# Turning twelve head outputs by 32x32 blocks through DRAM instead of TensorE transposes, in an RWKV-7 / HGRN2 mixer layer

## The chip, the cores and the metric

The kernel runs on one core of a Trainium2 chip. The metric is the device time of one execution in microseconds (us). The kernel before takes 1044.72 us, the median of 3 runs (1044.42 to 1045.22).

## What is computed

One layer of a streaming encoder over 512 frames of 2048 channels. One input projection feeds two groups of heads, their gated outputs are concatenated, and one output projection, a residual and a layer norm follow:

```python
proj = einsum('btd,dc->btc', x, w_in)            # 512 x 2048 by 2048 x 8320
rw = token_shift(proj[..., :RWKV_COLS], shift_mu)
o_rwkv = rwkv7(rw)      # 16 heads of 64 = 8 pairs: r, k, v, z, decay, a
o_hgrn = hgrn2(proj[..., RWKV_COLS:])    # 8 heads of 128: q, f, i, g
y = einsum('btc,cd->btd', concat([o_rwkv, o_hgrn]), w_out)
out = layer_norm(ALPHA * x + y) * ln_w + ln_b
```

The ends of the two branches matter here. In RWKV the recurrence's output `o` is normalized over each head of 64, scaled and shifted by `gn_w` and `gn_b`, gets a bonus `bv` added, and is multiplied by `silu(z)`. In HGRN2 the output is divided by its root mean square over the head of 128 and multiplied by `g_norm_w` and `silu(g)`. Everything is float32.

## The kernel before, in words

**Products.** A float32 product is made of three passes in the fp32r format: each operand is split into a high part and a rest, and `three` (L485) issues high by high, high by rest and rest by high, each 128x128 by 128x512, into one PSUM tile. The weights arrive as 156 blocks `wr` of 512 KB from `w_all`, two buffers; ACT makes the high part `wh` (L361) and DVE the rest `wl` (L371), half a block at a time, three buffers each. These products are the main stream of TensorE (PE in the profile). First come the units of the input projection in the order of `_order()`, then the output projection.

**Side work.** The recurrences run beside the main stream: after each product `three` calls `plan.pump()`, which looks at queues of Python generators (preparation and turning of a pair, groups, scans, finishes, HGRN heads, stores). Each generator yields one instruction at a time. `Plan` keeps an estimated clock for each engine and issues an instruction when its estimated inputs are ready; `room(...)` waits for a free buffer, `landed(...)` for operands that a PE instruction needs and for a free PSUM bank `mix`. The order that results is fixed when the program is built, each engine then runs its own part of it in order, waiting on semaphores where an input is late. So the planner's estimates set the order, and the chip's times only decide who waits. Side work on PE comes in two sorts: plain fp32 with all 128 rows and columns ("whole"), and small tiles ("narrow"); PE leaves the main stream for such a group and goes back to it.

**The ends, before.** `rwkv_finish(S, p)` for pair p normalizes the output `o_all`, a tile `t` with 128 frames by 4 blocks of 128 channels. Gating needs channels on the partitions, so four PE transposes (`tr`, L352, against the identity in `cst`) write it to a PSUM tile `po`. One DVE instruction `stt` (L380) makes `g = po * gn_w/2 + bv`; a Tanh, and two more, apply the gate z. `hgrn_out` ends in the same way: the normalized output `o2` (a `t` tile too) goes through four transposes to `pn`, and one `stt` makes `g = pn * (g_norm_w/2) * gate`. `put_gated` hands g on: for pairs 0 to 5 and heads 0 to 5 it is stored in DRAM (`spill<-g`) and read again for the output projection; pairs 6, 7 and heads 6, 7 stay in SBUF.

**Turning through DRAM.** The kernel has a second way to transpose, `turned(dst, src, tmp, rows)`, which it uses for `bk` and `v` in `rwkv_turn` and, for heads 0 to 5, for the keys in `hgrn_out`: DVE transposes each 32x32 block within itself (`dtr`, L390) into `tmp`; one DMA writes `tmp` to a DRAM tile `far`; `rows` DMAs read `far` back so that the blocks change places, each to 32 partitions. All these DMAs are issued by SyncE (SP) through `send` (L327), in one order with the weight loads. Before each the generator waits until the planner's SP clock is no more than 0.2 us ahead, and it counts 4 us for the write and 4 us for the last read. The result stands in the order "p (a c j)": block row a, block column c, 32 elements j, and was so far put in plain order by an ACT copy.

Of the kernel before, what the change touches and what calls it, by code (L numbers as in the profile page):

```python
# [11 lines left out]
ALU = mybir.AluOpType  # L12
# [3 lines left out]
P = 128  # L16
# [241 lines left out]
def mixer_kernel(ctx, tc, head, x_r, w_all, par, up, ln_wb, consts, hmask, out):  # L258
# [11 lines left out]
    def nm(s):  # L270
        uid[0] += 1
        return f"{s}{uid[0]}"
# [8 lines left out]
    def st(tag, shape, dt=F32):  # L281
        return spool.tile(shape, dt, tag=tag, name=nm(tag), bufs=BUFS[tag])

    def take(tag, shape=(P, T), dt=F32):

        if not plan.free(tag):
            raise RuntimeError(f"no room: {tag}")
        slot = min(plan.slots[tag])
        plan.slots[tag].remove(slot)
        if tag in PBUFS:  # L290
            t = ppool.tile(list(shape), dt, tag=tag, name=nm(tag), bufs=PBUFS[tag])
            plan.banks.add(t.tensor.name)
        else:
            t = st(tag, list(shape), dt)
        name = t.tensor.name
        plan.busy[name] = (slot[1], None)
        tags[name] = tag
        return t

    def drop(*tiles):  # L300
        for t in tiles:
            name = t.tensor.name
            plan.slots[tags.pop(name)].append((plan.used.get(name, plan.count), plan.busy[name][0]))

    def room(**need):

        return lambda: all(plan.free(tag, n) for tag, n in need.items())

    def has(S, *names):
        return lambda: all(n in S for n in names)  # L310

    def landed(*tiles, n=0):

        names = [getattr(t, "tensor", t).name for t in tiles]

        def test():
            now = plan.clock["pe"] + plan.LEAD
            if not plan.free("mix") or min(plan.slots["mix"])[1] + 0.15 > now:
                return False
            return all(n in plan.ready and plan.seen(n, "pe") <= now for n in names)  # L320

        test.batch = n
        return test

    def send(o, i, cost=0.44):

        nc.sync.dma_start(o, i)  # L327
        plan.clock["sp"] = max(plan.clock["sp"], plan.clock["pe"]) + cost


    def size(ap):
        n = 1
        for s in ap.shape[1:]:
            n *= s
        return n
# [15 lines left out]
    def tr(o, i):  # L351
        return Op([("pe", 0.11, lambda: pe.transpose(o, i, ident))], [i], [o])  # L352
# [14 lines left out]
    def dve_op(reads, o, f, n=None, per=0.00104, base=0.07):  # L367
        return Op([("dve", base + (n or size(o)) * per, f)], reads, [o])
# [10 lines left out]
    def stt(o, a, s, b, f1, f2):  # L379
        return dve_op([a, b], o, lambda: dve.scalar_tensor_tensor(o, a, s, b, f1, f2), per=0.00113,  # L380
                      base=0.085 if o.shape[0] == P else 0.25 if size(o) == C else 0.165)

    def red(o, i):
        return dve_op([i], o, lambda: dve.tensor_reduce(o, i, AX.X, ALU.add), size(i))
# [4 lines left out]
    def dtr(o, i):  # L389
        return dve_op([i], o, lambda: dve.transpose(o, i), per=0.0019)  # L390
# [25 lines left out]
    def blocks(t, n):  # L416

        return t.rearrange("p (a c j) -> p a c j", a=4, c=n)

    def turned(dst, src, tmp, rows=4):  # L420

        far = dpool.tile([P, rows, size(tmp) // rows], F32, tag=nm("far"), name=nm("far"))
        yield dtr(tmp.rearrange("p b c j -> p c b j"), src)
        yield lambda: by_now(tmp)
        yield lambda: plan.clock["sp"] <= plan.clock["pe"] + 0.2
        send(far, tmp.rearrange("p b c j -> p b (c j)"))
        there = plan.busy[tmp.tensor.name] = (plan.clock["sp"] + 4.0, "dma")
        for b in range(rows):
            yield lambda: there[0] <= plan.clock["pe"] and plan.clock["sp"] <= plan.clock["pe"] + 0.2
            send(dst(b).rearrange("i a c j -> i a (c j)"), far[:, b].rearrange("(a i) x -> i a x", a=4))  # L430
        plan.ready[dst(0).tensor.name] = (plan.clock["sp"] + 4.0, "dma")
# [58 lines left out]
    def by_now(t):  # L490

        n = t.tensor.name
        return n in plan.ready and plan.seen(n, "pe") <= plan.clock["pe"] + plan.LEAD
# [79 lines left out]
    HW0, HA0, HKA, HRK, HGW, HGB, HHW, HOKA = range(8)  # L573

    def hcol(i, p):

        return half[:, i, p : p + 1]
# [362 lines left out]
    def rwkv_finish(S, p):  # L940

        o_all = S["o"]
        yield room(sm=1, ksq=1)
        og = o_all.rearrange("p j (h i) -> p (j h) i", i=64)
        sm = take("sm", [P, 3, 8])
        sq = take("ksq", [P, 8, 64])
        yield red(sm[:, 0], og)
        yield ts(sm[:, 0], sm[:, 0], 1.0 / 64, None, ALU.mult)
        yield tt(og, og, sm[:, 0, :, None].to_broadcast([P, 8, 64]), ALU.subtract)
        yield act(sq, og, AF.Square)  # L950
        yield red(sm[:, 1], sq)
        yield ts(sm[:, 1], sm[:, 1], 1.0 / 64, GN_EPS, ALU.mult, ALU.add)
        yield rsqrt(sm[:, 2], sm[:, 1])
        yield tt(og, og, sm[:, 2, :, None].to_broadcast([P, 8, 64]))
        drop(sm, sq)
        yield has(S, "z", "bv")
        yield room(g=1, ksq=1)
        g = take("g")
        sz = take("ksq")
        z = S["z"]  # L960
        yield landed(o_all)
        po = take("mix")
        for j in range(4):
            yield tr(po[:, j * P : j * P + P], o_all[:, j])
        yield act(sz, z, AF.Tanh, scale=0.5)
        yield stt(g, po, hcol(HGW, p), S["bv"], ALU.mult, ALU.add)
        drop(po)
        yield stt(z, sz, 1.0, z, ALU.add, ALU.mult)
        yield stt(g, g, hcol(HGB, p), z, ALU.add, ALU.mult)
        drop(z, S["bv"], S["ot"], sz)  # L970
        put_gated(p, g)
# [17 lines left out]
    def tiles(t):  # L989
        return t.rearrange("p (c t) -> p c t", t=P)  # L990
# [110 lines left out]
    def hgrn_out(S, h, q, k, dt_, dg, tot, tots):  # L1101

        yield room(g=1)
        g = take("g")
        kt = state = tiles(k)[:, 0:3]
        if h < 6:
            yield room(ksq=1)
            tmp = take("ksq")
            g4 = blocks(g[:, : 3 * P], 3)
            yield from turned(lambda b: g4[32 * b : 32 * b + 32], kt, blocks(tmp[:, : 3 * P], 3))  # L1110
            drop(tmp)
            yield act(kt.rearrange("p c (a j) -> p c a j", j=32), g4.rearrange("p a c j -> p c a j"), AF.Copy)
        else:
            yield landed(k)
            ps = take("mix")
            for t in range(3):
                yield tr(ps[:, t * P : t * P + P], k[:, t * P : t * P + P])
            yield copy(kt, tiles(ps)[:, 0:3])
            drop(ps)
        yield has(S, "i")  # L1120
        yield room(rs=1)
        i_all = S["i"]
        hs = slice(h % 4 * P, h % 4 * P + P)
        yield landed(i_all, k)
        ps = take("mix")
        for t in range(3):
            yield mm(ps[:, t * P : t * P + P], kt[:, t], i_all[:, t, hs])
        yield copy(state[:, 0], ps[:, :P])
        for t in (1, 2):
            yield stt(state[:, t], state[:, t - 1], tot[:, t : t + 1], ps[:, t * P : t * P + P], ALU.mult, ALU.add)  # L1130
        drop(ps, *tots)
        yield landed(dg, k, q)
        po = take("mix")
        for t in range(4):
            o = po[:, t * P : t * P + P]
            yield mm(o, dg[:, t], i_all[:, t, hs], stop=(t == 0))
            if t:
                yield mm(o, q[:, t * P : t * P + P], state[:, t - 1], start=False)
        o2 = q
        yield act(o2, po, AF.Square)  # L1140
        rs = take("rs", [P, 8])[:, :4]
        yield red(rs, tiles(o2))
        yield ts(rs, rs, 1.0 / P, 4.0 * RMS_EPS, ALU.mult, ALU.add)
        yield rsqrt(rs, rs)
        yield tt(tiles(o2), tiles(po), rs[:, :, None].to_broadcast([P, 4, P]))
        drop(po, k, dt_, rs)
        S["used"]()
        yield landed(o2)
        pn = take("mix")
        for j in range(4):  # L1150
            yield tr(pn[:, j * P : j * P + P], o2[:, j * P : j * P + P])
        yield has(S, "g")
        yield stt(g, pn, hcol(HHW, h), S["g"], ALU.mult, ALU.mult)
        drop(S["g"], pn, o2)
        put_gated(8 + h, g)

    def silu2(ps, put):
# [459 lines left out]
    for t in range(4):  # L1617
# [14 lines left out]
        for i in range(2):  # L1632
            c = slice(i * T // 2, i * T // 2 + T // 2)
# [85 lines left out]
```

## Time and profile before

| what | value |
|---|---|
| median of 3 runs | 1044.72 us |
| the profiled execution | 1044.08 us, span 1042.3 us |
| PE busy | 1033.4 us, 99% of the span |
| DVE busy | 760.9 us, 73% |
| ACT busy | 439.0 us, 42% |
| POOL busy | 42.4 us, 4% |
| granted PE clock | full in all 40 slices |
| DMA | 123.46 MB, 118 GB/s on average |

The span goes from the first to the last instruction; the execution's time is 1.8 us longer. In the rows of the profile a line such as `L485 PE MATMUL main<-xl,wh` names the source line, the engine, the operation and the tiles out<-in without their buffer numbers. PEld is the loading of the stationary operand, which overlaps PE. SPq is SyncE issuing DMAs. Matmuls are pipelined: one that is listed with 0.39 us is followed by the next after about 0.23 us, so the sum of their durations says less than the steps from start to start.

### The profile page before, as it was taken

How to read it: one execution, taken by the hardware profiler on the slowest of the kernel's cores; microseconds unless marked ns; L12 is line 12 of the kernel's file. 1: busy time of each engine (PE TensorE's matmuls, PEld its weight loads, DVE VectorE, ACT ScalarE, POOL GpSimd, SP SyncE). 2: the span in 40 equal slices, each digit the busy share in tenths (PEclk: the TensorE clock that was granted, in tenths of full speed). 3: DMA queues.
4: the chain of work that ended last, by engine and by line, in shares of the span. 5: the costliest groups of instructions: out<-in, count | busy, mean ns of one | idle time of the engine just before them, and what ended most of it. 6: DMA issues, size and time to landing. Idle time of an engine off the chain costs nothing.

```text
span 1042.3 us, 19372 instructions
## 1 busy us (share of the span) xinstructions
PE 1033.4 (99%) x7708; PEld 854.4 (82%) x7708; DVE 760.9 (73%) x1614; ACT 439.0 (42%) x816; POOL 42.4 (4%) x77
## 2 busy tenths in 40 slices
PE   9999999999999999999999999999999999999997
PEld 7888887888888888888888888888888888888885
DVE  7477987678679878678997656866997886525556
ACT  6445334545343355355243344534335444223321
POOL 0000001001000000100001000100001011000000
PEclk9999999999999999999999999999999999999999
DMA  9134432232434322234542323243532245445613
GB/s 334 52 94 133 148 116 84 77 112 71 137 107 147 122 63 88 76 106 141 151 130 82 91 71 110 92 121 113 152 101 69 77 161 185 143 129 161 207 58 131
DMA packets 48618, 123.46 MB, mean 118 GB/s; under 512 B 8720, under 2 KB 17424, under 8 KB 48400
## 3 DMA queue, kind: packets, MB, share of 16 engines
q1 hardware_dynamic: 48384, 122.03, 37.3%
q8 instruction: 60, 0.98, 0.4%
q14 instruction: 30, 0.25, 0.1%
q10 hardware_dynamic: 144, 0.20, 0.1%
HBM read 107.39 MB, written 14.81 MB: 117 GB/s over the span
## 4 chain that ended last, share of the span: by engine, by line
PE 94%; DVE 2%; ACT 1%; DMA 1%; issue 1%; SPq 0%; DVEq 0%; ACTq 0%
PE main L485 71%; PE mix L348 10%; PE mix L485 8%; PE main L1244 3%; PE main L348 1%; PE mix L352 1%; DVE wl L371 1%; DMA q<-head 0%; DMA q<-far 0%; DVE inv L380 0%; DVE inv L371 0%; DVE t L371 0%; ACT L362 0%; DVE big L390 0%; ACT t L362 0%
## 5 line engine op out<-in xcount | busy, mean ns | idle before, releaser
L485 PE MATMUL main<-xh,wl 128*128 128x512 f32 x864 | 340.9, 395 | 0.0
L485 PE MATMUL main<-xl,wh 128*128 128x512 f32 x864 | 339.8, 393 | 0.0
L485 PE MATMUL main<-xh,wh 128*128 128x512 f32 x864 | 339.8, 393 | 0.0
L361 ACT ACTIVATE wh<-wr 128x512 fp32r<-128x512 f32 x299 | 186.3, 626 | 228.6 <-PE main L485 159.3
L371 DVE TENSOR_TENSOR wl<-wr,wh 128x512 fp32r<-128x512 f32 x299 | 203.7, 683 | 75.9 <-ACT wh L361 74.1
L485 PEld LDWEIGHTS main<-xl,wh 128*128 128x128 f32 x864 | 162.3, 188 | 33.6
L485 PEld LDWEIGHTS main<-xh,wl 128*128 128x128 f32 x864 | 162.4, 188 | 33.0
L485 PEld LDWEIGHTS main<-xh,wh 128*128 128x128 f32 x864 | 162.4, 188 | 32.8
L485 PE MATMUL main<-wh,xh 128*128 128x512 f32 (+1 forms) x262 | 102.3, 390 | 0.2 <-ACT t L362 0.2
L485 PE MATMUL main<-wl,xh 128*128 128x512 f32 (+1 forms) x262 | 102.3, 391 | 0.0
L485 PE MATMUL main<-wh,xl 128*128 128x512 f32 (+1 forms) x262 | 102.1, 390 | 0.0
L485 PEld LDWEIGHTS main<-wh,xh 128*128 128x128 f32 x262 | 49.2, 188 | 10.7 <-ACT t L362 0.6
L485 PEld LDWEIGHTS main<-wl,xh 128*128 128x128 f32 x262 | 49.2, 188 | 10.1 <-DVE wl L371 0.3
L485 PEld LDWEIGHTS main<-wh,xl 128*128 128x128 f32 x262 | 49.2, 188 | 9.8
L362 ACT ACTIVATE t<-main,om 128x512 f32<-128x512 f32 x33 | 22.4, 685 | 56.8 <-PE main L485 46.5
L371 DVE TENSOR_TENSOR inv<-inv,inv 64x30 f32<-64x30 f32 (+14 forms) x120 | 38.5, 321 | 3.0
L371 DVE TENSOR_TENSOR inv<-inv 64x30 f32<-64x30 f32 (+14 forms) x120 | 38.4, 320 | 2.7
L361 ACT ACTIVATE t<-mix 64x128 f32<-64x128 f32 (+3 forms) x60 | 16.8, 280 | 53.7 <-DVE zz L371 25.6
L380 DVE SCALAR_TENSOR_TENSOR bd<-mix,pc,bd 64x64 f32<-64x64 f32 x112 | 31.7, 283 | 10.6 <-PE mix L348 8.5
L380 DVE SCALAR_TENSOR_TENSOR t<-main,pr,t 128x511 f32<-128x511 f32 x33 | 24.4, 745 | 20.4 <-ACT t L362 20.4
L371 DVE TENSOR_TENSOR t<-t,tot 128x256 f32<-128x256 f32 x96 | 37.2, 419 | 0.3
L362 ACT ACTIVATE t<-main 128x512 f32<-128x512 f32 x32 | 18.6, 595 | 36.9 <-PE main L485 36.8
(218 smaller groups left out, 1317.5 us busy)
## 6 DMA issues: line engine op xcount, KB each, us to landing
wr<-w_all SPq DMA_DIRECT2D x156, 512.0 KB, 3.6
q<-head SPq DMA_DIRECT2D x15, 448.0 KB, 5.9
far<-q SPq DMA_DIRECT2D x8, 512.0 KB, 5.1
q<-far SPq DMA_DIRECT2D x32, 128.0 KB, 3.6
g<-x_r SPq DMA_DIRECT2D x16, 256.0 KB, 4.0
spill<-g SPq DMA_DIRECT2D x12, 256.0 KB, 3.7
out<-q SPq DMA_DIRECT2D x12, 256.0 KB, 2.5
t<-spill SPq DMA_DIRECT2D x10, 256.0 KB, 4.1
```

What stands on the lines that cost most here:

```text
L348: return Op([("pe", cost, lambda: pe.matmul(o, l, r, start=start, stop=stop, **kw))], [l, r], [o], mode="narrow" if narrow else "main" if ...
L352: return Op([("pe", 0.11, lambda: pe.transpose(o, i, ident))], [i], [o])
L361: return "act", cost, lambda: sc_e.activation(o, i, f, scale=scale)
L362: return "act", cost, lambda: sc_e.activation(o, i, f, scale=scale, bias=bias)
L371: return dve_op([a, b], o, lambda: dve.tensor_tensor(o, a, b, f), base=0.16 if o.shape[0] < P and size(o) == C and o.tensor.name in tags e ...
L380: return dve_op([a, b], o, lambda: dve.scalar_tensor_tensor(o, a, s, b, f1, f2), per=0.00113, base=0.085 if o.shape[0] == P else 0.25 if s ...
L485: pe.matmul(ps, l, r, start=first and i == 0, stop=last and i == 2)
L1244: pe.matmul(pss[a], *ops, start=k == 0 and low == of == 0, stop=k == KT - 1 and low == 1)
```

## The change

For pairs 0 to 5 and heads 0 to 5 the four PE transposes are left out, and the PSUM tile with them. In their place `turned` moves the output through DRAM: one `dtr` of 128x512 on DVE into a buffer `ksq`, one DMA of 256 KB to `far`, four DMAs of 64 KB back, in pieces of 512 B, into the tile that held the output (`o_all` or `o2`). Gating reads the blocks where they lie: four `stt` of 128x128, one for each block row a, take the place of the one of 128x512, with a strided view of g and of the other operand. There is no ACT copy. Pairs 6, 7 and heads 6, 7 keep the old code.

```diff
@@ rwkv_finish
         drop(sm, sq)
+        far = p < 6
+        if far:
+            yield room(ksq=1)
+            tmp = take("ksq")
+            o4 = blocks(S["ot"], 4)
+            yield from turned(lambda b: o4[32 * b : 32 * b + 32], o_all, blocks(tmp, 4))
+            drop(tmp)
         yield has(S, "z", "bv")
         yield room(g=1, ksq=1)
         g = take("g")
         sz = take("ksq")
         z = S["z"]
-        yield landed(o_all)
-        po = take("mix")
-        for j in range(4):
-            yield tr(po[:, j * P : j * P + P], o_all[:, j])
+        if not far:
+            yield landed(o_all)
+            po = take("mix")
+            for j in range(4):
+                yield tr(po[:, j * P : j * P + P], o_all[:, j])
         yield act(sz, z, AF.Tanh, scale=0.5)
-        yield stt(g, po, hcol(HGW, p), S["bv"], ALU.mult, ALU.add)
-        drop(po)
+        if far:
+            c4, b4 = (t.rearrange("p (c a j) -> p c a j", a=4, j=32) for t in (g, S["bv"]))
+            for a in range(4):
+                yield stt(c4[:, :, a], o4[:, a], hcol(HGW, p), b4[:, :, a], ALU.mult, ALU.add)
+        else:
+            yield stt(g, po, hcol(HGW, p), S["bv"], ALU.mult, ALU.add)
+            drop(po)
@@ hgrn_out
-        yield landed(o2)
-        pn = take("mix")
-        for j in range(4):
-            yield tr(pn[:, j * P : j * P + P], o2[:, j * P : j * P + P])
-        yield has(S, "g")
-        yield stt(g, pn, hcol(HHW, h), S["g"], ALU.mult, ALU.mult)
-        drop(S["g"], pn, o2)
+        if h < 6:
+            yield room(ksq=1)
+            tmp = take("ksq")
+            o4 = blocks(o2, 4)
+            yield from turned(lambda b: o4[32 * b : 32 * b + 32], tiles(o2), blocks(tmp, 4))
+            drop(tmp)
+            yield has(S, "g")
+            c4, s4 = (t.rearrange("p (c a j) -> p c a j", a=4, j=32) for t in (g, S["g"]))
+            for a in range(4):
+                yield stt(c4[:, :, a], o4[:, a], hcol(HHW, h), s4[:, :, a], ALU.mult, ALU.mult)
+            drop(S["g"], o2)
+        else:
+...
```

The planner then makes another order. The rows below are those of the built programs, engine by engine; the number behind a tile's name is its buffer. At the first of the twelve places, about 216 us into the profiled execution, PE's order before is this (`t_961` is the normalized output of an HGRN head):

```order
L485 MATMUL main_2178<-xh_81,wl_2229 128x512
L485 MATMUL main_2178<-xh_82,wh_2228 128x512
L352 MATMUL mix_2300<-cst,t_961 128x128 x4
L485 MATMUL main_2178<-xl_98,wh_2228 128x512
L485 MATMUL main_2178<-xh_82,wl_2229 128x512
```

and with the change this:

```order
L485 MATMUL main_2178<-xh_81,wl_2229 128x512
L485 MATMUL main_2178<-xh_82,wh_2228 128x512
L485 MATMUL main_2178<-xl_98,wh_2228 128x512
L485 MATMUL main_2178<-xh_82,wl_2229 128x512
L485 MATMUL main_2178<-xh_83,wh_2228 128x512
```

The group of four transposes is gone and the main stream goes on. In the whole program 70 transposes become 22, PE leaves the main stream for whole work 77 times where it was 86, and one pair of narrow groups more than before stands together.

DVE at the same place, before (`g_2053` is the gated output, `bd` the state of the RWKV scan):

```order
L371 TENSOR_TENSOR t_961<-mix_2244,rs_2253 128x512
L380 SCALAR_TENSOR_TENSOR bd_2112<-mix_2284,pc_627,bd_2112 64x64 x2
L380 SCALAR_TENSOR_TENSOR bd_2114<-mix_2285,pc_894,bd_2114 64x64 x2
L371 TENSOR_TENSOR wl_2304<-wr_2160,wh_2303 128x512
L380 SCALAR_TENSOR_TENSOR g_2053<-mix_2300,half,t_2180 128x512
```

and with the change:

```order
L371 TENSOR_TENSOR t_961<-mix_2244,rs_2253 128x512
L380 SCALAR_TENSOR_TENSOR bd_2112<-mix_2284,pc_627,bd_2112 64x64
L390 STREAM_TRANSPOSE ksq_2288<-t_961 128x4x4x32
L380 SCALAR_TENSOR_TENSOR bd_2112<-mix_2284,pc_627,bd_2112 64x64
...
L413 COPY t_940<-mix_2416 64x128
L380 SCALAR_TENSOR_TENSOR g_2053<-t_961,half,t_2180 128x4x32 x4
L390 STREAM_TRANSPOSE ksq_2433<-t_1273 128x3x4x32
```

The block transpose stands where the output is ready, and the gating moves back by some twenty DVE instructions, three `wl` splits among them.

SP's queue there, before:

```order
L327 DMA wr_2308<-w_all 128x1024
L327 DMA spill<-g_2053 128x512
L327 DMA far_2317<-ksq_2316 128x384
L327 DMA wr_2384<-w_all 128x1024
L327 DMA up_2386<-up 128x256
```

and with the change:

```order
L327 DMA wr_2309<-w_all 128x1024
L327 DMA far_2289<-ksq_2288 128x512
L327 DMA up_2355<-up 128x256
L327 DMA t_961<-far_2289 32x4x128 x4
L327 DMA wr_2392<-w_all 128x1024
L327 DMA spill<-g_2053 128x512
```

A write and four reads of `far` now stand between two weight loads, and the store of g behind them.

More of the change, by code (lines that the diff above doesn't have):

```diff
@@ L1147, in hgrn_out @@
         S["used"]()
-        yield landed(o2)
-        pn = take("mix")
-        for j in range(4):
-            yield tr(pn[:, j * P : j * P + P], o2[:, j * P : j * P + P])
-        yield has(S, "g")
-        yield stt(g, pn, hcol(HHW, h), S["g"], ALU.mult, ALU.mult)
-        drop(S["g"], pn, o2)
+        if h < 6:
[10 more added lines that the diff above has]
+        else:
+            yield landed(o2)
+            pn = take("mix")
+            for j in range(4):
+                yield tr(pn[:, j * P : j * P + P], o2[:, j * P : j * P + P])
+            yield has(S, "g")
+            yield stt(g, pn, hcol(HHW, h), S["g"], ALU.mult, ALU.mult)
+            drop(S["g"], pn, o2)
         put_gated(8 + h, g)
```

## The prediction

> **What bounds the kernel now.** I read the busy times first, then the waits of PE, then the order of time around the transposes, and only then DVE and the DMA queue.
>
> ```profile
> span 1042.3 us, 19372 instructions
> PE 1033.4 (99%) x7708; PEld 854.4 (82%) x7708; DVE 760.9 (73%) x1614; ACT 439.0 (42%) x816; POOL 42.4 (4%) x77
> ```
>
> PE is busy all the time by this page, but a busy PE need not be a PE at its pace. So the waits of PE, all that it has:
>
> ```profile
> PE mix L348 <- ACT ksq L1461: 1.5, 1, 1.5
> PE mix L1194 <- DVE inv L1192: 1.1, 1, 1.1
> PE mix L348 <- DVE ksq L371: 0.5, 1, 0.5
> PE mix L348 <- DVE t L371: 0.4, 1, 0.4
> PE main L1244 <- ACT xh L361: 0.4, 1, 0.4
> PE main L485 <- ACT t L362: 0.2, 1, 0.2
> ```
>
> The columns are the total, how often, and the longest. They sum to 4.1 us; the first is in the norm at the end, the second at the start. Between them PE waits 1.5 us in a thousand. No row has PE waiting on `wl` or `wh`, the split weights. So the time is the length of PE's own program, and what is taken out of that program is won, as long as nothing new makes PE wait.
>
> **What the transposes cost.** The group of all 70:
>
> ```profile
> L352 PE MATMUL mix<-cst,t 128*128 128x128 f32 x70 | 10.4, 272 | 0.0
> ```
>
> One transpose is listed with 272 ns. That is not what it adds. The order of time on PE around the first place:
>
> ```profile
> 215.74 0.40 PE L485 MATMUL main<-xh,wl 128*128 128x512 f32 x1
> 215.97 0.39 PE L485 MATMUL main<-xh,wh 128*128 128x512 f32 x1
> 216.20 0.60 PE L352 MATMUL mix<-cst,t 128*128 128x128 f32 x4
> 216.56 0.48 PE L485 MATMUL main<-xl,wh 128*128 128x512 f32 x1
> 216.87 0.40 PE L485 MATMUL main<-xh,wl 128*128 128x512 f32 x1
> 217.11 0.40 PE L485 MATMUL main<-xh,wh 128*128 128x512 f32 x1
> ```
>
> From start to start a product takes 0.23 us (215.74 to 215.97). With four transposes between, the products from 215.97 to 217.11 take 1.14 us for three steps. Three plain steps of 0.232 are 0.70. So the group costs 0.44 us: 0.36 for the four, and 0.08 by which the first product behind them is followed late (216.56 to 216.87 is 0.31). Of the twelve places that the change touches, ten look like this. At the other two the transposes share their trip with a state product:
>
> ```profile
> 626.62 0.60 PE L352 MATMUL mix<-cst,t 128*128 128x128 f32 x4
> 627.05 0.61 PE L348 MATMUL mix<-bd,q 128*128 128x128 f32 x4
> ```
>
> Without them the state product would start where they start, 0.43 us earlier; so sharing a trip saves nothing. **Term 1: 10 by 0.44 and 2 by 0.43 us, 5.3 us less.**
>
> As bounds: by busy time the 70 transposes have 10.4 us, 0.149 each, and 48 of them 7.1 us; by 0.36 a group, if the slow first step stayed in some other form, 4.3 us. I take 5.3, since it comes from starts.
>
> [...]
>
> **Other moves in PE's order.** Whole groups that meet save nothing (just shown). Narrow groups that meet save something:
>
> ```profile
> 145.45 0.39 PE L485 MATMUL main<-wh,xl 128*128 128x512 f32 x1
> 145.77 0.89 PE L348 MATMUL mix<-q,t 128*32 128x48 f32 x64
> 146.59 0.50 PE L485 MATMUL main<-wh,xh 128*128 128x512 f32 x1
> 146.92 0.40 PE L485 MATMUL main<-wl,xh 128*128 128x512 f32 x1
> ...
> 376.69 0.39 PE L485 MATMUL main<-xh,wl 128*128 128x512 f32 x1
> 377.01 0.89 PE L348 MATMUL mix<-q,t 128*32 128x48 f32 x64
> 377.83 2.08 PE L348 MATMUL mix<-big 64*64 64x64 f32 x64
> 379.84 0.50 PE L485 MATMUL main<-xh,wh 128*128 128x512 f32 x1
> ```
>
> Alone the first kind costs 0.32 to enter (145.45 to 145.77) where a plain step has 0.23, and 0.33 to the second product (146.59 to 146.92); together the second group follows the first after 0.82, as the product did alone (145.77 to 146.59), so an entry of 0.09 and an exit of 0.10 are paid once instead of twice. The order has one such meeting more than before. **Term 2: 0.2 us less.** The last 330 rows of PE's order are the same as before but for numbers, so the output projection and the norm keep their length.
>
> **What is added beside PE.** On DVE:
>
> ```profile
> L390 DVE STREAM_TRANSPOSE ksq<-t 128x512 f32<-128x512 f32 x8 | 5.6, 698 | 0.0
> L380 DVE SCALAR_TENSOR_TENSOR g<-mix,half,t 128x512 f32<-128x512 f32 x16 | 12.0, 748 | 2.6 <-PE mix L352 2.2
> L380 DVE SCALAR_TENSOR_TENSOR t<-t,tot,mix 128x128 f32<-128x128 f32 x16 | 5.5, 345 | 2.4 <-ACT t L361 2.1
> ```
>
> Each unit adds a block transpose of 0.70 and four gatings of 128x128. The nearest row for one of these has 0.345 and an operand in PSUM; a quarter of the old one would be 0.187. So they cost between 0.75 and 1.38 in place of 0.75, and a unit adds 0.70 to 1.33 us, twelve of them 8 to 16 us. I take 15, since a small instruction keeps its fixed part. DVE has 281 us idle (1042.3 less 760.9), and the units lie in three stretches, of which these two are the fuller:
>
> ```profile
> 435.00:515.00 80.00, 79.54 (x422) 65.86 (x421) 65.87 (x115) 38.77 (x62) 6.74 (x6) 1.00 0.41 122
> 665.00:745.00 80.00, 80.00 (x432) 66.08 (x428) 61.86 (x107) 32.63 (x53) 3.92 (x4) 1.00 0.40 120
> ```
>
> The third pair of figures is DVE's: 65.9 of 80 and 61.9 of 80. Four units in each add some 5 us: the fuller goes from 82% to 89%. It is hidden; if that cover were gone, 15 us.
>
> The gating waits for the last read, and DVE runs in order, so the `wl` splits queue behind a late one, and PE behind them. The order puts it about twenty instructions behind the block transpose. In DRAM the way takes one write and four reads:
>
> ```profile
> wr<-w_all SPq DMA_DIRECT2D x156, 512.0 KB, 3.6
> q<-far SPq DMA_DIRECT2D x32, 128.0 KB, 3.6
> far<-ksq SPq DMA_DIRECT2D x8, 256.0 KB, 4.0
> g<-far SPq DMA_DIRECT2D x24, 48.0 KB, 3.4
> ```
>
> The write of 256 KB is in the list with 4.0 us; a read of 64 KB lies between 3.4 (48 KB) and 3.6 (128 KB). With the issues that is about 9 us per unit. Nobody on PE waits for a gated output of pairs 0 to 5 or heads 0 to 5 until the output projection, since it is stored and read again. **Term 3: nothing**, between 0 and 2.7 less gain (the second rival).
>
> On SP each DMA has an issue, the first row (least, median and longest ns), and each set of reads waits for its write, with weight loads queued behind:
>
> ```profile
> L327 SPq DMA_DIRECT2D g<-far x24: 326/432/1754, 195.5 to 635.5; - x24
> ...
> SPq L327 <- DVE wl L371: 517.6, 107, 13.0
> SPq L327 <- DMA far<-q: 18.4, 7, 4.7
> SPq L327 <- DMA far<-ksq: 7.3, 2, 3.7
> ```
>
> 60 more issues of 0.43 us are 26 us of SP. It waits 517.6 us for `wl`, for a buffer to come free, so it has the time. What it waited for `far` in the 22 turns that the kernel has already (25.7 us in 9 waits) put no wait on PE. I count nothing.
>
> **Sum.** 1044.08 for the profiled execution less 5.3 and 0.2 is 1038.6. The median is 0.64 above that execution, so 1039.2 us. A measurement of this kernel can tell some 0.2% from no change, 2.1 us; the forecast is 0.5%.
>
> **The rivals.**
>
> *Part of it comes back in small waits on PE (chance 0.12).* The order is made by estimates, and gating in strips or a late read can differ from them by a few tenths. The waits on DVE that PE had amid the program were 0.4 and 0.5 us; if six of the twelve units bring one of 0.45, that is 2.7 us, and the time is 1041.9. For it speaks DVE's fullest stretch; against it that the turns which the kernel has already, eight of them with a block transpose of this very size, brought none.
>
> *SP's order makes the weights late, and the kernel slower (0.05).* A read of `far` stands at the head of SP's queue until its write has landed, and a weight load behind it starts late; with two `wr` buffers PE then waits for `wl`. The mean wait on `far` is 25.7/9, or 2.9 us. It decides from 0.63 us per unit: twelve of those eat the 5.5 us and 2.1 more. At 1 us uncovered per unit the time is 1051.2, at the whole 2.9 it is 1074. Against it: no wait of PE on `wl` in the trace of before, with waits of up to 4.7 us on SP. [...]
>
> *The freed time isn't used (0.05).* The change does what it says, 22 transposes are left in the built order, but PE waits at the end for a chain of the recurrences that has not become shorter: 1044.7. Against it: the last transposes come some 6 products earlier in the main stream (of 3964), not later.
>
> *A transpose costs its whole listed time (0.02).* 48 by 0.272 is 13.1 us, and the time 1031.6. The starts speak against it.
>
> **Chances and range.** The forecast has 0.76, with its bounds from 1037.6 (7.1 us less by busy time) to 1040.4 (4.3 less). With the first rival to 1041.9 the range holds 0.88, less what falls beyond these bounds. Faster by over 0.2%: forecast, first and last rival, 0.90. Within: 0.05. Slower: 0.05.
>
> **What would show it.** In the changed kernel's profile: 22 transposes in L352's group with the same 272 ns; main products that go on at 0.23 us at the twelve places; the waits of PE still at about 4 us; DVE's busy time near 776; 20 instead of 8 block transposes of 128x512 into `ksq`; 48 reads of `far` in pieces of 64 KB, landing after 3.4 to 3.6 us. A row of PE waiting on `wl`, or on DVE in the first column of its waits with more than 2 us, would make the sum wrong, as would a `far` wait of SP that grows beyond some 50 us with ACT waiting for `wr`.

## The result and the profile after

| | before | changed |
|---|---|---|
| median of 4 runs each, us | 1044.74 (1044.42 to 1045.22) | 1039.24 (1038.64 to 1039.73) |
| ratio, 95% interval | | 0.9947 (0.9929 to 0.9964) |
| the profiled execution, us | 1044.08 | 1039.73 |

The forecast was 1039.2. From profile to profile the gain is 4.35 us, between the medians 5.5: the changed kernel's profiled execution was the slowest of its four. The head of its page, to be read against that of before:

```profile
span 1037.9 us, 19437 instructions
PE 1026.9 (99%) x7660; PEld 849.8 (82%) x7660; DVE 766.4 (74%) x1642; ACT 447.6 (43%) x836; POOL 42.7 (4%) x77
```

PE has 48 instructions and 6.5 us of busy time less (1033.4 before), and it is still the bound. All waits of PE, in us in total, number, longest:

```profile
PE mix L348 <- ACT ksq L1486: 1.5, 1, 1.5
PE mix L1219 <- DVE inv L1217: 1.1, 1, 1.1
PE mix L348 <- DVE ksq L371: 0.8, 1, 0.8
PE main L1269 <- ACT xh L361: 0.8, 1, 0.8
PE main L485 <- ACT t L362: 0.7, 1, 0.7
PE mix L348 <- issue: 0.7, 1, 0.7
PE mix L348 <- DVE t L371: 0.4, 1, 0.4
```

They sum to 6.0 us where it was 4.1. None is on `wl` or `wh`, none on the gated strips. But the middle ones are new or longer, by 1.9 us in all. Not all of that is the change's. Up to the first of the twelve places, at 216 us, every engine has the same order in both kernels, and 0.9 of the 1.9 us lies ahead of it: 0.4 on `xh` at 8 us (0.77 for 0.37), and 0.5 (0.69 for 0.19) here:

```profile
136.50 0.50 PE L485 MATMUL main<-wh,xh 128*128 128x512 f32 x1 [0.69 <-ACT t L362]
```

The number in brackets is the idle time ahead and what ended it. At this same instruction a kernel without any of the new DMAs (the one with doubled transposes, below) waited 0.8 us. So these 0.9 us are scatter of one execution. Behind the first place PE's waits grew by 1.0 us, in two rows: `ksq` at 753 us (0.83, where before had 0.46 at 496), and a wait of 0.7 at 817 us for which the profile shows no cause (issue).

PE's order of time at the first of the twelve places, where four transposes stood before (start, duration, instruction):

```profile
216.19 0.39 PE L485 MATMUL main<-xh,wh 128*128 128x512 f32 x1
216.42 0.39 PE L485 MATMUL main<-xl,wh 128*128 128x512 f32 x1
216.65 0.40 PE L485 MATMUL main<-xh,wl 128*128 128x512 f32 x1
```

Every step is 0.23 us; the gap of 0.44 is gone. The groups that the change touches:

```profile
L352 PE MATMUL mix<-cst,t 128*128 128x128 f32 x22 | 3.2, 272 | 0.0
L390 DVE STREAM_TRANSPOSE ksq<-t 128x512 f32<-128x512 f32 x20 | 14.0, 702 | 0.2
L380 DVE SCALAR_TENSOR_TENSOR g<-t,half,t 128x128 f32<-128x128 f32 x48 | 14.6, 342 | 3.8 <-DMA t<-far 3.7
L380 DVE SCALAR_TENSOR_TENSOR g<-mix,half,t 128x512 f32<-128x512 f32 x4 | 3.0, 748 | 0.8 <-PE mix L352 0.6
```

The block transposes add 8.4 us to DVE (14.0 less 5.6), the gating 5.6 (14.6 and 3.0 in place of 12.0): 14.0, where 15 was taken. Yet DVE's total rose by 5.5 only. The planner gives some copies to ACT or to DVE, whichever it thinks free, and gave more of them to ACT. In these rows the figures behind the bar are the group's busy time in us, the mean of one in ns, and the idle time ahead of it. The copies into `big`, by line, before:

```profile
L413 DVE COPY big<-mix 64x512 f32<-64x512 f32 (+1 forms) x8 | 4.7, 588 | 7.0 <-ACT big L361 3.8 <-PE mix L348 3.1
L361 ACT ACTIVATE big<-mix 32x256 f32<-32x256 f32 (+1 forms) x24 | 11.4, 476 | 11.9 <-PE mix L348 11.4 <-DVE big L413 0.3
```

and after:

```profile
L413 DVE COPY big<-mix 64x512 f32<-64x512 f32 x2 | 1.4, 682 | 2.9 <-PE mix L348 2.9
L361 ACT ACTIVATE big<-mix 32x256 f32<-32x256 f32 (+1 forms) x30 | 14.4, 479 | 10.7 <-PE mix L348 10.3
```

Thirty-two copies both times; six have gone over. In the whole program it is twenty: DVE's copies at L413 fall from 89 to 69, or by 5.6 us, and ACT's instructions at L361 rise from 626 to 646, by 8.7 us. ACT's total rose by 8.6 us, with nothing in the change that asks for ACT.

The DMA issues (KB each, median us from issue to landing), and SP's waits on `far`:

```profile
far<-ksq SPq DMA_DIRECT2D x20, 256.0 KB, 4.2
t<-far SPq DMA_DIRECT2D x48, 64.0 KB, 3.4
q<-far SPq DMA_DIRECT2D x32, 128.0 KB, 4.5
```

```profile
SPq L327 <- DMA far<-ksq: 32.5, 11, 3.8
SPq L327 <- DMA far<-q: 13.0, 5, 4.7
```

The new reads land in 3.4 us, as forecast. SP waits 45.5 us for `far` in place of 25.7. The reads of `q`, which were there already, land after 4.5 us where it was 3.6. That the new traffic delays them is not shown: only 4 of the 32, those at 688 us, had a new transfer in flight with them, and other old reads landed as before or sooner (`zz<-far` 4.2 us both times, `g<-far` 3.2 for 3.4).

### The profile page after: what moved, and what is told of

Read it like the earlier page. It is cut to its first block, busy times and chain, and to the rows that moved or that the text cites. A ratio compares the mean times of both kernels' runs of the same rounds, so it can differ in the third digit from the quotient of the medians.

```text
span 1037.9 us, 19437 instructions
## 1 busy us (share of the span) xinstructions
PE 1026.9 (99%) x7660; PEld 849.8 (82%) x7660; DVE 766.4 (74%) x1642; ACT 447.6 (43%) x836; POOL 42.7 (4%) x77
## 4 chain that ended last, share of the span: by engine, by line
PE 94%; DVE 3%; DMA 1%; issue 1%; ACT 1%; SPq 0%; DVEq 0%; ACTq 0%
PE main L485 71%; PE mix L348 10%; PE mix L485 8%; PE main L1269 3%; PE main L348 1%; DMA q<-far 1%; DVE wl L371 1%; DVE inv L371 1%; DMA q<-head 1%; DVE inv L380 0%; SPq L327 0%; ACT t L362 0%; DVE t L371 0%; PE mix L352 0%; DVE big L390 0%
## 5 line engine op out<-in xcount | busy, mean ns | idle before, releaser
L361 ACT ACTIVATE wh<-wr 128x512 fp32r<-128x512 f32 x299 | 186.1, 626 | 218.0 <-PE main L485 160.5
L361 ACT ACTIVATE t<-mix 64x128 f32<-64x128 f32 (+2 forms) x67 | 18.6, 279 | 62.5 <-PE mix L348 27.8
```

Of the source, the lines that this page charges most:

```text
L361: return "act", cost, lambda: sc_e.activation(o, i, f, scale=scale)
```

## The experiments

My theory was that of the prediction: the time is PE's own program, a group of four transposes costs it 0.44 us, and the way through DRAM is hidden. Its rivals: a transpose costs its listed 0.272 us and the DRAM way gives part of that back; or the DRAM way has a price that the new order happens to avoid. Each kernel ran beside the kernel before on the same chip, with a median of 1044.89 us for that in the first four experiments (transposes twice, each half, transposes kept), 1044.53 in the next four (reads later, also with the transposes kept; reads twice; all sixteen) and 1044.23 in the last four (those with 19 tiles).

### More transposes, no DRAM way

The kernel before, with each of the twelve groups issued twice over (the same edit stands in `hgrn_out`, with h for p):

```diff
-        for j in range(4):
+        for j in (range(4) if p > 5 else (0, 0, 1, 1, 2, 2, 3, 3)):
             yield tr(po[:, j * P : j * P + P], o_all[:, j])
```

> The kernel before, with each of the 48 transposes of the six pairs and six heads issued twice in a row into the same place (118 transposes in all). It prices a transpose inside a trip that PE makes anyway. The four in a row lasted 0.60 us with 0.272 for the last, so a step of 0.11 us: 48 by 0.11 is 5.3 us more, about 1050.0 us, if nothing is paid for entering and leaving such a trip. If the 0.08 us behind the trip is a price of the trip, a transpose has 0.09 us and the time is 1049.0 us. By the listed 0.272 us each it is 13.1 us more, 1057.8 us.

Measured: 1049.56 us, ratio 1.0044 (1.0031 to 1.0056). That is 4.67 us for 48 more transposes, 0.097 each; the 13.1 us of the listed time are excluded. PE's order of time at the first place:

```profile
216.95 1.03 PE L352 MATMUL mix<-cst,t 128*128 128x128 f32 x8
217.82 0.61 PE L348 MATMUL mix<-bd,q 128*128 128x128 f32 x4
```

Eight start within 0.87 us, 0.109 each. A transpose is listed with 273 ns here (mean of the 118 of this run), and what is paid is 0.1 us.

### Each half alone

Only the six pairs go by DRAM, or only the six heads:

```diff
-        if h < 6:
+        if h < 0:
```

```diff
-        far = p < 6
+        far = p < 0
```

> Only the six pairs are turned through DRAM; the eight heads keep their transposes (46 transposes left instead of 70). Theory (PE's own program sets the time, a group of four transposes is worth 0.44 us): 6 groups by 0.44 is 2.6 us less; in this order no two narrow groups meet, where before has one such meeting, so 0.2 us come back: 2.4 us less than before, about 1042.3 us, ratio 0.9977. Rival (the gain of the whole change came from the new order as a whole, or from a PSUM bank that is not taken any more, not from the transposes' time on PE): no fixed share per group, so anything else between 1039 and 1045 us.

> Only the six heads are turned through DRAM; the eight pairs keep their transposes (46 left). Theory: again 6 by 0.44 us less 0.2 us for the meeting of narrow groups that is missing in this order: 2.4 us less than before, about 1042.3 us. With the run for the pairs alone the two gains add up to 4.9, and the whole change has 5.5 because its order has two such meetings. Rival (the order as a whole, or the PSUM bank): the two do not add up to the whole.

Measured: heads alone 1043.19 us, ratio 0.9981 (0.9972 to 0.999), a gain of 2.0 us by the ratio (1.7 between the medians) where 2.4 was expected; that fits. Pairs alone 1045.12, ratio 1.0002 (0.9993 to 1.0011): no gain. That is a miss. The halves give 1.8 us together by their ratios, and the whole gave 5.5, so the gain is no sum of equal shares.

Where did the pairs' 2.4 us go? PE's waits have risen from 4.1 to 6.4 us. Counted from start to start, the places with a wait take about 3.7 us longer than before, which more than eats the 2.4 (that would make 1.3 more; the span is 0.9 longer). The longest new wait, in PE's order of time:

```profile
706.72 0.50 PE L348 MATMUL mix<-ksq,ones_r 128*128 128x512 f32 x1 [1.25 <-ACT ksq L361]
```

What ACT did ahead of that:

```profile
704.57 1.06 ACT L361 ACTIVATE q<-q 128x1024 f32<-128x1024 f32 x1 [6.37 <-DMA q<-far]
...
706.05 0.61 ACT L361 ACTIVATE ksq<-t 128x512 fp32r<-128x512 f32 x1
```

and SP:

```profile
690.31 0.43 SPq L327 DMA_DIRECT2D far<-q  x1
695.28 2.24 SPq L327 DMA_DIRECT2D q<-far  x2
698.02 0.35 SPq L327 DMA_DIRECT2D wr<-w_all  x1
698.47 0.85 SPq L327 DMA_DIRECT2D q<-far  x2
```

Read backwards: PE wants `ksq`, the operand of a sum of squares that has nothing to do with the turned tiles. ACT would make it, but in ACT's order an older turn's copy `q<-q` stands ahead, and it waits 6.37 us for a read. That read came out of SP late, behind its write and a weight load, and took 5.6 us to land. Before, the four reads of that turn had no weight load among them and landed within 2.9 us. So nobody on PE waits for a turned tile; PE waits for something unrelated that stands behind one, on an engine that runs in order. This cause is read from the trace, for this one wait of the several; no run undid it, and which of the new transfers put the weight load there is not shown.

### The same PE work, with the DRAM way

The changed kernel, with the old four transposes still issued for each of the twelve (their result is not used; the same lines stand in `hgrn_out`):

```diff
         if far:
+            yield landed(o_all)
+            po = take("mix")
+            for j in range(4):
+                yield tr(po[:, j * P : j * P + P], o_all[:, j])
+            drop(po)
             yield room(ksq=1)
```

> The changed kernel, with the four PE transposes per group put back as dead work: they write a PSUM tile that nobody reads, and the way through DRAM and the gating by strips stay. 70 transposes again. Theory: PE gets its 5.3 us back and the DRAM way costs nothing, so the time is that of before but for the meetings of narrow groups: 1039.2 + 5.3 = 1044.5 us. Rival (the DRAM way or the gating costs some us on PE's path, which the saved transposes more than pay): the sum is the same 5.3 above the changed kernel, but PE's waits, if they are more than 2 us above those of before, show it. Rival (the new order brings the gain, not the missing transposes): the time stays near 1039 to 1041 us.

Measured: 1048.75 us, ratio 1.0043 (1.003 to 1.0055), 3.9 us slower than before with PE's instructions the same. A miss, and the one that counts: here what the change brings besides is not hidden. The run doesn't part the DRAM way from the new order that comes with it, nor from its later start, since the transposes now stand ahead of the block transpose. And against the changed kernel the 48 transposes cost 9.5 us here, twice the 4.7 of the first experiment: what such an edit costs depends on the order that it leads to. PE's waits:

```profile
PE main L485 <- DVE t L380: 1.9, 2, 1.8
PE main L485 <- ACT t L362: 1.2, 2, 0.7
```

Before had 0.2 us of these two kinds; of the second row 0.5 is the wait at 136 us, ahead of the first place. Both are the main stream waiting for a PSUM bank to be emptied into a `t` tile. The kernel has 18 `t` tiles, and a normalized output that goes through DRAM holds its tile until the last strip is gated.

### The reads placed later

If PE waits because strips are gated too early, then counting 6 us instead of 4 for the reads should help:

```diff
-        plan.ready[dst(0).tensor.name] = (plan.clock["sp"] + 4.0, "dma")
+        plan.ready[dst(0).tensor.name] = (plan.clock["sp"] + 6.0, "dma")
```

> The changed kernel, with the planner's count for the last read of a turn raised from 4 to 6 us: who uses a turned tile is placed later in its engine's order, nothing else is edited. The runs before gave waits of PE of 0.3 to 1.9 us where ACT or DVE stood in its order at an instruction that waits for a read of far, with work for PE queued behind it. Theory (the DRAM way costs PE a few tenths here and there, by being used earlier in the order than it lands): PE's waits fall from 6.0 us to some 4.5 and the time to 1037.5 to 1038.5 us. Rival (the waits have to do with the order in general, not with landing): waits and time as in the changed kernel within 0.5 us, or worse. Rival (gated outputs now come too late for the output projection): above 1040 us with a wait at the end.

> The changed kernel with the transposes kept as dead work, and the planner's count for the last read at 6 us. With 4 us it took 1048.75, 4 us more than the 1044.5 of PE's sum, and PE had waits of 1.8 and 0.7 us behind ACT and DVE instructions that had waited for far. Theory (late landing in an order of instructions that can't overtake): most of the 4 us go, 1044.5 to 1046. Rival (the DRAM way costs PE about 4 us through SP and the weight loads, or through DVE's time): no change, 1048 to 1049.5.

Measured: 1048.35 us, ratio 1.0039 (1.0025 to 1.0053), and with the transposes kept 1055.44, ratio 1.0104 (1.0089 to 1.0118). Both lost: 9.1 us against the changed kernel, 6.7 against the kernel with the transposes kept. The theory of a late read fell, and the trace shows what stood in its place. PE's order of time in the first of the two:

```profile
463.72 0.40 PE L485 MATMUL main<-xh,wl 128*128 128x512 f32 x1
471.96 0.80 PE L485 MATMUL main<-xh,wh 128*128 128x512 f32 x1 [7.84 <-DVE t L380]
472.55 0.63 PE L485 MATMUL main<-xl,wh 128*128 128x512 f32 x1
472.98 0.63 PE L485 MATMUL main<-xh,wl 128*128 128x512 f32 x1
...
475.92 0.40 PE L485 MATMUL main<-xh,wh 128*128 128x512 f32 x1
```

and DVE's, at the end of that wait:

```profile
470.89 0.35 DVE L380 SCALAR_TENSOR_TENSOR g<-t,half,t 128x128 f32<-128x128 f32 x1
471.15 1.41 DVE L380 SCALAR_TENSOR_TENSOR t<-main,pr,t 128x511 f32<-128x511 f32 x2
```

One wait of 7.84 us, and it ends when the fourth strip of a gating is done and the projection's result leaves its PSUM bank. Near 465 us several turns stand together. My reading: with each held 2 us longer in the planner's account, the `t` tiles run out, the planner lets the projection's evacuations (the copies out of PSUM) wait for a gating, and the main stream stops with all its banks full. Then the cost is not who waits for the result, but who waits for the buffer that it is kept in.

### A longer way, and one more tile

The test of that: hold the tiles longer in another way, by issuing each of the four new reads twice, once with 18 `t` tiles and once with 19; and the kernel with the transposes kept, with 19. The kernels with the reads placed later were not run with 19.

```diff
-        for b in range(rows):
+        for b in list(range(rows)) * times:
...
-            yield from turned(lambda b: o4[32 * b : 32 * b + 32], o_all, blocks(tmp, 4))
+            yield from turned(lambda b: o4[32 * b : 32 * b + 32], o_all, blocks(tmp, 4), times=2)
```

```diff
-    BUFS = {"t": 18, "q4": 6, "big": 1, "inv": 2, "ia": 1, "g": 4, "wr": 2, "wh": 3, "wl": 3, "pf": 1,
+    BUFS = {"t": 19, "q4": 6, "big": 1, "inv": 2, "ia": 1, "g": 4, "wr": 2, "wh": 3, "wl": 3, "pf": 1,
```

> The changed kernel with each of the 48 new reads of far issued twice (96 reads, 3.1 MB more, some 20 us more issue time of SP, and each gated output ready about 3 us later). Theory (the DRAM way's traffic and SP's time are hidden, and only the place of the user in the order counts): the same time within the scatter of an order, 1038.5 to 1041. Rival (SP's queue and the weight loads behind it are what the DRAM way costs): PE waits for wl or wh, and the time rises by 4 us or more, to 1043 or above.

> Every new read of far issued twice, as in the run that took 1059.1 us, with 19 buffers t. Buffer theory: the wait of 10.1 us of PE on the move out of PSUM goes, and with it its slow aftermath of some 2 us; what is left are waits of ACT and DVE for far: 1040 to 1044 us. Rival (SP's queue, its 96 reads and the weight loads behind them cost the 20 us): 1053 us or more.

> The changed kernel with its transposes kept as dead work, and 19 buffers t in place of 18. With 18 it took 1048.75. New theory (buffers): a turned output and the tiles that its gating reads hold their t buffers for the whole way through DRAM; where three turns stand together, about 465 us into the run, none is free, the next projection can't be moved out of its PSUM bank, and PE waits until a gating has ended. With one buffer more the wait there (1.8 us, then another of 0.7) is gone and the time falls to that of before: 1044.3 to 1046, and then the way through DRAM itself costs PE under 1.5 us. Rival (the waits are those of ACT and DVE for late reads, buffers or not): 1047.5 to 1049.5.

Measured: reads twice 1059.1 us, ratio 1.0145 (1.0125 to 1.0164), far over what the theory had expected of it. The rival of that run had more than 1043, by weights that come late; but no wait of PE there is on `wl` or `wh`. With one more tile 1049.39, ratio 1.0039 (1.0025 to 1.0052): 9.7 us come back from a single buffer, and the order that it leads to. PE's wait with 18 tiles,

```profile
PE main L485 <- DVE t L380: 10.1, 1, 10.1
```

is gone with 19; what is left at the head of the list is

```profile
PE mix L348 <- ACT ksq L361: 4.8, 2, 2.7
```

and that is the other mechanism, met again. ACT, in its order of time:

```profile
548.43 1.06 ACT L361 ACTIVATE q<-q 128x1024 f32<-128x1024 f32 x1 [5.50 <-DMA q<-far]
549.39 0.61 ACT L361 ACTIVATE ksq<-t 128x512 fp32r<-128x512 f32 x1
```

The expected 1040 to 1044 was missed. These two waits, with the slow products behind each (4.8 us, and some 3 by the steps; last section), are most of what is left against the changed kernel: the tile was one of two costs.

With the transposes kept, 19 tiles gave 1047.96 us, ratio 1.0031 (1.0019 to 1.0043). The wait of 1.8 us is gone, but the time is still 3.7 above that of before, where 1044.3 to 1046 was expected; it lies where the rival had it (1047.5 to 1049.5, waits that have nothing to do with buffers). In its place stand small waits of 0.2 to 0.6 us at several places and trips from the main stream that take longer; I count some 2.6 us of such from the profile, and can't name one cause for them. So the tile was not most of it here.

### All sixteen

```diff
-        far = p < 6
+        far = p < 8
...
-        if h < 6:
+        if h < 8:
```

> All eight pairs and all eight heads are turned through DRAM, so pairs 6, 7 and heads 6, 7 too (6 transposes of keys left). By PE's sum alone 16 groups by 0.44 and the meeting of narrow groups, 7.2 us less than before: 1037.6. Theory (the gain holds only where some 9 us of latency are covered): outputs 14, 6, 15, 7 are the last operands of the output projection's first part, and in this order the last side work on PE stands 51 products later than in the changed kernel; PE then waits for a split of a late output, some 3 to 8 us, and the time is 1041 to 1046. Rival (the latency is covered to the end): 1037 to 1038.5.

Measured: 1054.52 us, ratio 1.0093 (1.0079 to 1.0108). The direction was expected, the size not. Pairs and heads 6 and 7 are the last ones, and the output projection takes them straight from SBUF, so nothing is left to hide their way. PE:

```profile
PE main L485 <- ACT xh L361: 12.5, 2, 7.7
```

SP and DVE at the first of the two:

```profile
870.72 0.33 SPq L327 DMA_DIRECT2D far<-ksq  x1
...
880.33 1.76 SPq L327 DMA_DIRECT2D t<-far  x4
```

```profile
884.32 1.14 DVE L380 SCALAR_TENSOR_TENSOR g<-t,half,t 128x128 f32<-128x128 f32 x4 [8.08 <-DMA t<-far]
```

From the issue of the write to the gating it is 13.6 us, not 9: the reads were issued 9.6 us after the write. For 6.5 us of that SP issued nothing: its weight load at 873.54 ends at 873.87, and the reads, which need the write, stand behind it. In the changed kernel a write of this kind lands after 4.2 us in the median. A load of 2 MB, `big<-ln_wb`, had been issued 2 us ahead of the write; in the changed kernel this load takes 8.7 us to land. That it held the write up is likely, but no run shows it. At the second wait nothing of the sort stands by: from the write (896.27) to the gating (902.15) it is 5.9 us, and PE waits 7.7, since nothing covers even that.

### Seven pairs, and the change with 19 tiles

Pair 6 turned through DRAM as well, with 19 tiles (pair 7 and heads 6, 7 stay as they were); and the changed kernel with 19 tiles and nothing else:

```diff
-        far = p < 6
+        far = p < 7
```

> The changed kernel with 19 buffers t and pair 6 turned through DRAM as well (18 transposes left). Buffer theory: PE's sum is 13 by 0.44 and two meetings of narrow groups more than before, 6.1 us less: 1038.6 us, and no new wait, since the last side work stands only 12 products later than in the changed kernel. Rival (pair 6 has no cover left before the output projection, as with all sixteen): PE waits for a split of a gated output and the time is above 1040.

> The changed kernel with 19 buffers t and nothing else. Buffer theory: the changed kernel just had room, without a wait at 465 us, so one buffer more brings little: PE's sum says 0.2 us less by one more meeting of narrow groups, 1038 to 1039.5 us. Rival (the order moves the time by several us whatever the room): outside 1037 to 1041.

Measured: 1038.67 us, ratio 0.9944 (0.9932 to 0.9956), and 1038.97, ratio 0.9947 (0.9935 to 0.9959). Both as expected, and neither can be told from the change itself (0.9947). A spare tile brings nothing where none is missing. Both have another order than the changed kernel, and the same gain.

## Why the prediction was right, and how far

**PE's program is the time: right.** No engine took its place. Doubling the transposes cost time, leaving them out gained it, at nearly the same price each: 0.097 and 0.115 us (5.5/48). That price is not found again in every order: put back into the changed kernel the 48 cost 9.5 us (9.0 with 19 tiles), and leaving out the 24 of the pairs alone gained nothing.

**Term 1, 5.3 us for the transposes: right.** The steps at the places are 0.23, the group keeps its 272 ns, and the doubled groups bound the price at 0.067 to 0.122 us each by their interval (3.2 to 5.9 us), where 0.110 was used. The rival with the whole listed time is out.

**Term 2, 0.2 us: not tested.** It is smaller than what two medians can tell apart.

**Term 3, nothing for the DRAM way: nearly right for this order, wrong as a rule.** This is the step whose argument failed. From the first place on, PE's waits are 1.0 us longer in the profiled execution, so by the terms it should have gained 5.5 less 1.0, or 4.5, there. It gained 5.3 (the 4.35 from profile to profile, and the 0.9 lost ahead of the first place), so 0.8 us of gain has no term and stays open. That the median falls on the forecast to 0.1 us is partly luck: a cost and a gain that were not in the sum nearly cancel, and the runs scatter over 1.1 us. The reason given was that nobody on PE waits for a gated output. That is true, and not enough. With the same PE instructions the DRAM way and its order cost 3.9 us (1048.75), pairs alone lost all their gain, and 2 us more in the planner's account of a read cost 9.1. Nor did the kernel's old turns, which had brought no wait, prove it for the new ones: they had fewer to share SP, ACT and the `t` tiles with.

**The first rival, small waits on PE: it happened in part.** Its price for the change was 2.7 us, the profile shows 1.0 behind the first place: 0.4 more on a `ksq` that DVE makes for other work, not on the gated strips as I had it, and 0.7 without a cause that the profile shows. The first has the chain of the pairs alone behind it: at 748 us ACT's copy `q<-q` had waited 3.6 us for its read, DVE then 1.6 us for ACT, and `ksq` came late. In all ACT waited 10.8 us for reads of `q`, where it was 5.7 before.

**The rival by SP's order: its road was wrong, its sign possible.** No list of PE's waits here has one on `wl` or `wh` of more than 0.31 us, so late weights decided nothing. But three other ways of spending more time between `far` and gating did end slower than before: 1048.35 and 1059.1 by way of `t` tiles and of ACT's order, 1054.52 because the output projection waited for the gated outputs themselves. SP's own sign, a `far` wait of over 50 us, was not reached (45.5).

**DVE near 776: wrong.** The added work was sized well (14.0 for 15), the total was not (766.4), because a planner that chooses between engines moved twenty copies to ACT. The same choice changes ACT's order, where the late copies stand.

**What stays open:** why the kernel with the transposes kept is 3.7 us slower than before even with 19 tiles, what made the wait of 0.7 at 817 us, where the 0.8 us of gain without a term come from, and whether pairs alone would gain if the copy `q<-q` stood later on ACT. No run was made for these.

## What to carry to other kernels

Price a small PE instruction by the steps from start to start around it, not by its listed duration (here 0.1 us by the doubled groups, with 0.27 listed). When work moves from a short way to a long one, "nobody needs the result soon" covers only half: list as well which buffers the long way holds meanwhile, and which instructions stand behind the late one on each engine that runs in order (with the pairs alone `ksq` stood on ACT behind a wait of 6.37 us). Time such a change by halves and with more of itself too, since a gain of half a per cent (0.9947) can stand beside losses of the same size (1.0043 with the transposes kept) that the present order just avoids.

## What was not expected of the hardware

Some long waits of PE cost more than their length here. After the wait of 7.84 us above, products follow each other at 0.43 us instead of 0.23: the nine steps from 471.96 to 475.92 take 3.96 us, 1.9 more than nine of 0.23. The mean granted clock of TensorE, as a share of full speed, is 0.997 in that execution, where that of before has 1.000. A much shorter wait did the same. PE's order of time of the reads issued twice with 19 tiles:

```profile
547.54 0.39 PE L485 MATMUL main<-xh,wl 128*128 128x512 f32 x1
550.06 0.50 PE L348 MATMUL mix<-ksq,ones_r 128*128 128x512 f32 x1 [2.13 <-ACT ksq L361]
...
551.12 0.57 PE L485 MATMUL main<-xh,wh 128*128 128x512 f32 x1
...
552.34 0.63 PE L485 MATMUL main<-xh,wh 128*128 128x512 f32 x1
...
554.77 0.39 PE L485 MATMUL main<-xh,wh 128*128 128x512 f32 x1
```

From start to start that gap has 2.52 us, and the nine steps from 551.12 to 554.77 take 3.65 us in place of 2.07; the mean granted clock of that execution is 0.996. The second wait of that kernel, 2.69 us at 709.89, was followed by such steps as well: the seven from 711.82 to 714.81 take 2.99 us, 0.43 each. A wait of 1.76 us, with the transposes kept and 18 tiles, was not; PE's order of time:

```profile
469.82 0.51 PE L485 MATMUL main<-xh,wh 128*128 128x512 f32 x1 [1.76 <-DVE t L380]
470.16 0.40 PE L485 MATMUL main<-xl,wh 128*128 128x512 f32 x1
470.40 0.40 PE L485 MATMUL main<-xh,wl 128*128 128x512 f32 x1
```

There the products go on at 0.24 and 0.23 us from the second on, and from start to start that gap has 2.15 us (467.67 to 469.82). What decides between the two cases no run here parted.

The other surprise: how long one and the same transfer takes to land. Writes of 256 KB to `far` took 4.2 us in the median with the change; with all sixteen the reads behind one of them were issued 9.6 us after it. The `q` reads of 128 KB landed after 3.6 us before and 4.5 us with the change, and it was behind such reads that ACT stood in the two kernels above. What decides it in each case no run here parted.
